# A DeltaNet layer's squares of q summed by column-group products, one head's transposes a unit later, and a selection matrix built earlier

## The chip, the cores and the metric

The kernel runs on one core of a Trainium2 chip. The time is the device time of one execution in microseconds (us), the median of several runs. The core's engines, as the profile names them: PE is TensorE (matmuls and transposes), PEld its weight loads, DVE is VectorE, ACT is ScalarE, POOL is GpSimd, SP is SyncE, which issues most of the DMAs.

## The reference

A decoder trunk of two layers over 512 positions of 1024 channels, float32. Layer 0 mixes tokens with a gated DeltaNet (8 heads of 128), layer 1 with a Conformer convolution. Each layer then attends to a fixed memory of 256 positions and applies a squared-ReLU MLP of width 4096. What the change touches, cut:

```python
def l2_normalize(x):
    return x * lax.rsqrt(jnp.sum(x * x, axis=-1, keepdims=True) + 1e-6)

# gated_deltanet
qkv = jax.nn.silu(causal_depthwise_conv(qkv, w_conv))
q = l2_normalize(q) * (DN_HEAD_DIM ** -0.5)
k = l2_normalize(k)
o = chunk_gated_delta_rule(q, k, v, g, beta)
o = o * lax.rsqrt(jnp.mean(o * o, axis=-1, keepdims=True) + RMS_EPS) * out_norm

# conformer_conv
u = h @ w_pw1 + b_pw1
u = u[..., :D_MODEL] * jax.nn.sigmoid(u[..., D_MODEL:])
c = causal_depthwise_conv(u, w_dw) + b_dw          # width 31
c = jax.nn.silu(layer_norm(c, ln_g, ln_b))
return c @ w_pw2 + b_pw2
# every sub-layer has rms_norm(h, g) before it
```

The division by q's length isn't applied to q. It goes into the RMS norm of o, as an addend: `o_norm` adds q's sum of squares (times a constant, in `ssq`) to the mean of o's squares before the root. So q's sums are needed only late.

## The kernel before, in words

Activations are kept transposed: a tile holds 128 channels (partitions) by 512 positions. Each weight half (128x1024) is loaded by SP, split into a high part `wh` by ACT (line 253) and a low part `wl` by DVE (or, for some, POOL) (line 73), and used in three matmuls (`mm3`, lines 300 to 302). Large activation tiles are split the same way (`xh`, `xl`). So TensorE waits whenever a split is late.

The order on each engine is written by a planner that takes the code's order as priority, and starts what is ready by its own model of times. Most tiles of 128x512 come from one pool of 69 slots (`slot`), the 8 PSUM banks from another (`psum`), and an instruction isn't ready before its slot is free. `keep_in_program_order` (also `pin`) ties an instruction behind all that was written before it for its engine; `issue_after` ties a block behind one instruction.

**DeltaNet.** `run(mains, sides)` issues a list of TensorE units (`mains`, half a projection tile each, some 2.7 to 3 us) and after each the small works planned for it (`sides`; `S.at(unit, rank, work)`). Units 4 to 33 are k, q, z and v of the first four heads (`gq` 0), 34 to 65 of the other four (`gq` 1), 66 to 73 the memory's keys (K's units), 74 to 81 its values (V's units), 82 to 89 half the output projection. The works that matter here:
- `q2` makes q times k of a head (units `Q2`) and keeps q as `self.QT[h]`, channels by positions.
- `q3` (units `Q3`) transposes q of a head in four matmuls into PSUM (`qt`), and ACT squares each of the four blocks with a running sum into a column of `ssq`, positions in the partitions. `norm_q` (units 33 and 62) adds an epsilon and scales.
- `fs_*` solve the triangular blocks on DVE; `mg_*` (units from 36 and from 68) merge them on TensorE.
- `tap_v`, `silu` make v of a head; `v2` transposes v (`vt`) and DVE scales it (`vb`). For `gq` 1 heads 4 to 6 go at unit 73, head 7 at unit 74. From unit 75 `rec` runs the recurrence, whose first matmul `vn` (unit 76) reads `vb`.
- `o_norm` (units 74 and 88) reads `ssq`.

The product `ab` at the start (line 1744) has four 32-column weights in TensorE's four column groups, each with a 128x512 tile.

**The first MLP's end and the conformer's start.** `mlp7(0)` forms its down projection in seven products per group of weights (`dn7`). Before the last group (`g == 3`) it calls `mid`, which splits the memory for layer 1 (`mem_gain`: `mh` by ACT, `ml` by DVE) and loads nine pieces of `taps`. `outs` then transposes the sums back (`hT`), adds the residual (`h`), splits it for the next norm (`parts`: `xh` by ACT, `xl` by DVE) and squares it (`Norm.square`), first for tiles 0 to 3 and, as `rest`, for 4 to 7, inside the conformer's first projection `pw_mm`. `norm.stat` multiplies the sum of squares by ones (`ssq`, line 442) at step `STAT` of the projection's eight, and ACT and DVE make `rb` from it, which `pw_ev` needs.

`sel`, made on DVE at the conformer's start from the identity, selects and sums rows in the layer norm after the convolution (`ln`).

Of the kernel before, what the change touches and what calls it, by code (L numbers as in the profile page):

```python
# [38 lines left out]
def tile_trunk(ctx, tc, xT, memT, x_d, mem_d, prm_d, adt_d, bdw_d, tap_d, fin_d, first_d, w_ab, w_kq, w_v, w_z, w_dno, w_pw1, w_pw2,  # L39
               w_q, w_k, w_vv, w_o, w_up, w_dn, yT):  # L40
    nc = tc.nc
    pe, act, dve, pool = nc.tensor, nc.scalar, nc.vector, nc.gpsimd
# [24 lines left out]
    def const(shape, s, dt=F32):  # L67
        return cp.tile(list(shape), dt, tag=s, name=s)
# [3 lines left out]
    def tt(e, o, a, b, op):  # L72
        r = e.tensor_tensor(out=o, in0=a, in1=b, op=op)  # L73
        if e is pool:
            last_pool[:] = [r]
        return r
# [4 lines left out]
    def ts(e, o, a, s1, op0, s2=None, op1=None):  # L81
        if op1 is None:
            return e.tensor_scalar(out=o, in0=a, scalar1=s1, scalar2=None, op0=op0)
        return e.tensor_scalar(out=o, in0=a, scalar1=s1, scalar2=s2, op0=op0, op1=op1)

    def c4(t):
        return t.rearrange("p (c i) -> p c i", c=4)
# [4 lines left out]
    def over_c(t, n=4):  # L92
        return t.unsqueeze(1).to_broadcast([P, n, t.shape[1]])
# [18 lines left out]
    def piece(e, i):  # L112
        e.dma_start(out=raw0[:, i * 256:(i + 1) * 256], in_=w_kq[0][:, i * 256:(i + 1) * 256])
# [11 lines left out]
    ident = const([P, P], "ident")  # L125
# [4 lines left out]
    for i in range(WARM):  # L130
# [5 lines left out]
    pool.affine_select(out=tri_gt, in_=ones, pattern=[[-1, P]], compare_op=ALU.is_gt, fill=0.0,  # L136
                       base=0, channel_multiplier=1)
    piece(act, 1)
    ones_r = const([P, P], "ones_r", F32R)
    pool.tensor_copy(ones_r, ones)  # L140
    tri_mid = const([P, P], "tri_mid")
# [58 lines left out]
    for kind, gq in DN_ORDER:  # L200
        for i in range(2):
            j = gq * 2 + i
# [202 lines left out]

    class Norm:
        def __init__(self, gname):
            self.g, self.acc, self.xs, self.n, self.side = gname, None, [], 0, None

        def add(self, t, h):  # L410
            self.parts(t, h)
# [6 lines left out]
            pin(stt(xl, h, pc(self.g, t), xh.bitcast(F32), ALU.mult, ALU.subtract))  # L418
            self.xs.append((xh, xl))

        def square(self, h, e=pool, side=False):
            sq = slot(s="sq")
            act.activation(sq, h, AF.Square)  # L423
            self.n += 1
            if side:
                if self.side:
                    tt(pool, self.side, self.side, sq, ALU.add)
                self.side = self.side or sq
                return
            if self.acc is None:  # L430
                self.acc = sq
            else:
                tt(dve if self.n == KT else e, self.acc, self.acc, sq, ALU.add)
            if self.n == KT:
                if self.side:
                    tt(dve, self.acc, self.acc, self.side, ALU.add)
                self.hl = split(self.acc, "sq")

        def stat(self):
# [28 lines left out]
    class DeltaNet:  # L468
# [196 lines left out]
            self.QT[h] = qT  # L665

        def q3(self, h):
            ps, sq = psum("qt"), slot(s="sqq")
            for c in range(4):
                cs = slice(c * P, (c + 1) * P)  # L670
                pe.transpose(ps[:, cs], self.QT[h][:, cs], ident)
            for c in range(4):
                cs = slice(c * P, (c + 1) * P)
                act.activation(sq[:, cs], ps[:, cs], AF.Square, accum_out=self.ssq[:, 4 * h + c:4 * h + c + 1])

        def norm_q(self, gq):
            v = self.ssq[:, 16 * gq:16 * gq + 16]
            ts(dve, v, v, EPS, ALU.add, EPS * P, ALU.mult)


        def fs_in(self, h):
# [291 lines left out]
    def mem_gain(layer, half):  # L973
        gn = f"xa_mem{layer}"
        if half == 0:
            mem["xs"] = []
        for j in (2 * half, 2 * half + 1):
            if layer == 1:
                m = mem["m"][j].rearrange("p (k t) -> p k t", k=2)
                tt(dve, m, m, over_c(mem["rs"][:, 0:256], 2), ALU.mult)  # L980
            mh = slot(F32R, "mh")
            ml = slot(F32R, "ml")
            for i in range(2):
                ks = slice(i * 256, (i + 1) * 256)
# [181 lines left out]
    def mlp7(layer, norm, hres, nxt=None, mid=None):  # L1166
# [123 lines left out]
        new = [None] * 8  # L1290

        def outs(tiles):
            todo = [(n, c, i) for n in range(2) for c in range(2) for i in tiles]
            pss = {i: psum("hT") for i in tiles}
            for n, c, i in todo:
                j = 2 * n + c
                pe.transpose(pss[i][:, j * P:(j + 1) * P], acc[n, 1 - i // 4, c][:, i % 4 * P:i % 4 * P + P], ident)
            for k, i in enumerate(tiles):
                hn = slot(s="h")
                tt(dve, hn, pss[i], hres[i], ALU.add)  # L1300
                new[i] = hn
                if k:
                    nxt.parts(i - 1, new[i - 1])
                if i > 5:
                    nxt.square(new[i - 2], side=True)
            nxt.parts(i, hn)
            for hn in new[0:4] if i == 3 else new[6:8]:
                nxt.square(hn, pool if i == 3 else dve)

        def final(n, m, c, held=None):  # L1310
            opens = n not in fin or fin[n][4][c] is None
# [92 lines left out]
    def taps(m, *pieces):  # L1404
        TAPS.setdefault(m, [])
        for i in pieces:
            t = slot(s="tap")
            nc.sync.dma_start(out=t, in_=tap_d[m - NTAP, i])
            TAPS[m].append(t)

    def conformer(norm, hres, nxt, rest):
        xs = norm.xs
        st, x16 = {}, {}
# [2 lines left out]
        Yp = [fsp.tile([P, 1024], F32, tag="fs", name=nm("cyp")) for _ in range(2)]  # L1416
        bias = slot(s="bdw")[:, 0:P]
        nc.sync.dma_start(out=bias, in_=bdw_d)
        sel = slot(s="sel")
        dve.tensor_reduce(out=sel[:, 128:160], in_=ident.rearrange("p (g t) -> p t g", g=4), op=ALU.add, axis=AX.X)  # L1420
        dve.tensor_reduce(out=sel[:, 160:164], in_=c4(ident), op=ALU.add, axis=AX.X)
        dve.tensor_copy(c4(sel[:, 0:128]), over_c(sel[:, 128:160]))
        own, same_t = over_c(sel[:, 160:164]), sel[:, 0:128]

        def pw_mm(i, hf):
# [242 lines left out]
        new = []  # L1668
# [21 lines left out]
    for i in range(4):  # L1690
        s = slice(i * 256, (i + 1) * 256)
# [30 lines left out]
    D = DeltaNet(n0)  # L1722
    D.decay_const(0)
    mains, S = [], Sides()
# [70 lines left out]
    for gq in range(2):  # L1795
        f0, nf = FS[gq]
        S.at(f0, 5, D.fs_begin, gq)
        for i in range(nf):
            S.at(f0 + i, 6, D.fs_steps, gq, i * 31 // nf, (i + 1) * 31 // nf)
        S.at(f0 + nf, 1, D.fs_end, gq)  # L1800
        for h in range(4 * gq, 4 * gq + 4):
            S.at(f0 + nf, 1, D.mg_a, h)
        S.at(f0 + 1, 7, D.norm_k, gq)
        S.at(f0 + nf + 2, 7, D.norm_q, gq)
        for i in range(4):
            h = 4 * gq + i
            S.at(f0 + nf - 4 + i, 5, D.mg_pre, h)
        a, b = (4 * gq, 4 * gq + 1), (4 * gq + 2, 4 * gq + 3)
        for j, (f, x, y) in enumerate(((D.mg_wy, a, ()), (D.mg_wy, b, a), (D.mg_te, a, ()), (D.mg_te, b, a), (D.mg_te, (), b))):
            S.at(MG[gq] + j, 1, f, x, y)  # L1810
        S.at(MG[gq] + 2, 1, D.mg_wy, (), b)
        for j, x in ((1, a), (2, b)):
            S.at(MG[gq] + j, 1.5, D.mg_u, x)
        for c in range(4):
            u = at["v", 4 * gq + 3] + V2[gq]
            if gq == 1:
                S.at(u, 3, D.v2, gq, c, (0, 1, 2))
                S.at(u + 1, 0, D.v2, gq, c, (3,))
        n = 0
        for c in range(4):  # L1820
            for step in range(3):
                S.at(REC[gq] + n, 0, D.rec, gq, c, step)
                n += 1
            S.at(REC[gq] + n + (c < 3 if gq == 1 else -(c == 1)), 5, D.o_gate, gq, c)
        S.at(ONORM[gq], 1, D.o_norm, gq)
    S.at(MSQ - 4, 7, mem_tok)
    for j in range(4):
        S.at(MSQ + j, 7, mem_square, j)
# [33 lines left out]
    h = []  # L1862
# [12 lines left out]
    n2 = Norm("mlp_norm0")  # L1875
    h = xattn(0, n1, h, n2)
    n3 = Norm("cv_norm")
    h, rest = mlp7(0, n2, h, n3, lambda: (mem_gain(1, 0), mem_gain(1, 1), taps(NTAP, *range(9))))
    n4 = Norm("xa_norm1")
    h = conformer(n3, h, n4, rest)  # L1880
    n5 = Norm("mlp_norm1")
# [3 lines left out]
    mlp7(1, n5, h)  # L1885


NSLOT = 69
NCV = 6
NRAW = 3  # L1890
RAWB = 6
# [21 lines left out]
ROOT_K = (32, 72)  # L1913
K2 = (15, 16, 18, 19, 45, 46, 49, 48)
Q2 = (18, 20, 22, 23, 48, 50, 50, 53)
Q3 = (24, 25, 27, 29, 55, 56, 57, 59)
FS = ((22, 9), (52, 8))
MG = (36, 68)
V2 = (10, 9)
# [6 lines left out]
TAPK = {0: 8, 1: 9, 2: 11, 3: 12}  # L1926
TAPQ = {0: 12, 4: 44}
TAPV = (37, 38, 39, 40, 69, 69, 70, 71)
STAT = 2
TAPS_U = (4,) * 7 + (6,) * 9 + (3,) * 8 + (0,) * 8  # L1930
TAPS_C = {4: 0, 5: 0, 6: 0, 7: 0}
SHARE = 5
# [113 lines left out]
```

## Time and profile before

| | us |
|---|---|
| median of 3 runs (1444.9 to 1445.53) | 1445.21 |
| the profiled execution | 1444.54 |
| its span, first to last instruction | 1442.8 |
| PE busy | 1432.4 |
| DVE busy | 1053.5 |
| ACT busy | 763.6 |
| POOL busy | 249.2 |

Lines of the profile give a start in us from the span's start, a duration in us, the engine, the source line (a helper such as line 73 or 79 stands for many callers), the operation, and out<-in by tile names. In brackets stands how long the engine was idle before and what released it. The duration of a matmul is longer than the step from one to the next, because they are pipelined.

### The profile page before, as it was taken

To read this page: it belongs to the slowest core of one execution; us is meant where nothing else is said; L and a number is where in the kernel's file an instruction comes from. 1 tells how busy PE (TensorE), PEld (TensorE's weight loads), DVE (VectorE), ACT (ScalarE), POOL (GpSimd) and SP (SyncE) were. 2 spreads that over 40 slices of the span, in tenths; PEclk is the share of its full clock that TensorE was granted. 3 is DMA by queue.
4 is the path that set the end of the run, shared out by engine and by line. 5 is a ranking of instruction groups with operands and counts; after the bars stand their busy time and mean duration, and the time that the engine had idled before them with its cause. 6 is when DMAs were issued, how large, how long until landed. Compare 5 with 4: busy or idle time off the path is not lost.

```text
span 1442.8 us, 20243 instructions
## 1 busy us (share of the span) xinstructions
PE 1432.4 (99%) x7670; PEld 1199.2 (83%) x7670; DVE 1053.5 (73%) x1600; ACT 763.6 (53%) x1322; POOL 249.2 (17%) x250
## 2 busy tenths in 40 slices
PE   9999999999999999999999999999999999999998
PEld 7888889888888888888888778888888888888886
DVE  6989888867555765767679899975555766767677
ACT  6767856655444454434355655564444544444354
POOL 1301200102113010010100478111112010010101
PEclk9999999999999999999999999999999999999999
DMA  8232225522214576575766448743215476675853
GB/s 300 73 117 75 70 92 162 195 84 88 74 40 127 153 177 175 141 206 131 198 165 217 141 147 244 252 139 99 73 49 141 117 182 169 149 206 135 222 150 88
DMA packets 71857, 207.80 MB, mean 144 GB/s; under 512 B 15440, under 2 KB 16592, under 8 KB 71760
## 3 DMA queue, kind: packets, MB, share of 16 engines
q1 hardware_dynamic: 60960, 169.22, 35.9%
q0 software_dynamic: 9792, 35.66, 14.5%
q10 hardware_dynamic: 1008, 1.64, 0.3%
q8 instruction: 60, 0.98, 0.3%
q14 instruction: 37, 0.30, 0.1%
HBM read 203.28 MB, written 3.21 MB: 143 GB/s over the span
## 4 chain that ended last, share of the span: by engine, by line
PE 91%; DVE 5%; ACT 2%; issue 1%; DMA 0%; POOL 0%; SPq 0%; DVEq 0%; ACTq 0%; POOLq 0%
PE up L302 8%; PE up L301 8%; PE up L300 8%; PE dn L1218 7%; PE dn L1217 7%; PE dn L1216 7%; PE h L300 3%; PE h L302 3%; PE h L301 3%; PE xo L301 2%; PE q L301 2%; PE xo L300 2%; PE q L300 2%; PE q L302 2%; PE xo L302 2%; PE pw L302 2%
## 5 line engine op out<-in xcount | busy, mean ns | idle before, releaser
L253 ACT CAST wh<-raw 128x1024 fp32r<-128x1024 f32 x259 | 271.6, 1051 | 345.0 <-issue 89.1
L73 DVE TENSOR_TENSOR wl<-raw,wh 128x1024 fp32r<-128x1024 f32 (+1 forms) x250 | 306.0, 1225 | 97.1 <-ACT wh L253 94.8
L300 PE MATMUL up<-xh,wh 128*128 128x512 f32 x512 | 199.7, 390 | 0.0
L302 PE MATMUL up<-xh,wl 128*128 128x512 f32 x512 | 199.3, 389 | 0.0
L301 PE MATMUL up<-xl,wh 128*128 128x512 f32 x512 | 199.2, 389 | 0.0
L302 PEld LDWEIGHTS up<-xh,wl 128*128 128x128 f32 x512 | 96.1, 188 | 19.9
L300 PEld LDWEIGHTS up<-xh,wh 128*128 128x128 f32 x512 | 96.1, 188 | 19.9
L301 PEld LDWEIGHTS up<-xl,wh 128*128 128x128 f32 x512 | 96.1, 188 | 19.9
L241 POOL DMA_DIRECT2D t<-w_dn x48 | 42.1, 914 | 367.5 <-DVE wl L73 269.6
L1216 PE MATMUL dn<-wh,ah 128*128 128x512 f32 (+1 forms) x260 | 100.5, 387 | 0.0
L1218 PE MATMUL dn<-wl,ah 128*128 128x512 f32 (+1 forms) x260 | 100.4, 386 | 0.0
L1217 PE MATMUL dn<-wh,al 128*128 128x512 f32 (+1 forms) x260 | 100.4, 386 | 0.0
L79 DVE SCALAR_TENSOR_TENSOR rl<-up,rb 128x512 f32<-128x512 f32 x64 | 44.1, 689 | 58.4 <-PE up L302 58.4
L253 ACT CAST wh<-t 128x1024 fp32r<-128x1024 f32 x44 | 46.4, 1054 | 55.0 <-PE dn L1217 43.7
L73 DVE TENSOR_TENSOR wl<-t,wh 128x1024 fp32r<-128x1024 f32 x44 | 53.6, 1223 | 28.7 <-ACT wh L253 28.6
L73 POOL TENSOR_TENSOR sq<-sq,sq 128x512 f32<-128x512 f32 x28 | 46.0, 1643 | 154.2 <-ACT sq L423 143.6
L1495 DVE SCALAR_TENSOR_TENSOR ca<-xn,prm,ca 128x512 f32<-128x512 f32 x85 | 64.1, 754 | 5.7 <-ACT ca L1492 3.4
L73 DVE TENSOR_TENSOR acc<-acc,dn 128x512 f32<-128x512 f32 x99 | 66.6, 682 | 1.0
L300 PE MATMUL h<-xh,wh 128*128 128x512 f32 x160 | 64.2, 401 | 0.0
L302 PE MATMUL h<-xh,wl 128*128 128x512 f32 x160 | 62.5, 390 | 0.0
L301 PE MATMUL h<-xl,wh 128*128 128x512 f32 x160 | 62.4, 390 | 0.0
L73 DVE TENSOR_TENSOR al<-u,ah 128x512 fp32r<-128x512 f32 x64 | 44.1, 688 | 21.4 <-ACT ah L359 21.4
(421 smaller groups left out, 3520.2 us busy)
## 6 DMA issues: line engine op xcount, KB each, us to landing
raw<-w_dn SPq DMA_DIRECT2D x68, 512.0 KB, 4.5
raw<-w_up SPq DMA_DIRECT2D x64, 512.0 KB, 4.8
t<-w_dn POOLq DMA_DIRECT2D x48, 512.0 KB, 6.4
tap<-tap SPq DMA_DIRECT2D x48, 256.0 KB, 6.2
raw<-w_pw SPq DMA_DIRECT2D x24, 512.0 KB, 4.6
raw<-w_dn POOLq DMA_DIRECT2D x20, 512.0 KB, 6.6
raw<-w_k SPq DMA_DIRECT2D x16, 512.0 KB, 4.1
raw<-w_vv SPq DMA_DIRECT2D x16, 512.0 KB, 6.1
```

The lines of the kernel that those rows point to most:

```text
L73: r = e.tensor_tensor(out=o, in0=a, in1=b, op=op)
L79: return dve.scalar_tensor_tensor(out=o, in0=a, scalar=s, in1=b, op0=op0, op1=op1)
L241: nc.gpsimd.dma_start(out=t, in_=a, accum_op=ALU.add)
L253: ins = [act.copy(h, raw)]
L300: pe.matmul(ps, wh, xh, start=first, stop=False)
L301: pe.matmul(ps, wh, xl, start=False, stop=False)
L302: pe.matmul(ps, wl, xh, start=False, stop=last)
L1216: pe.matmul(ps, xh, w[0][:, s], start=opens and k == 0, stop=False, skip_group_check=True)
L1217: pe.matmul(ps, xl, w[0][:, s], start=False, stop=False, skip_group_check=True)
L1218: pe.matmul(ps, xh, w[1][:, s], start=False, stop=k == 3, skip_group_check=True)
L1495: first["tap"] = dve.scalar_tensor_tensor(out=a, in0=src, scalar=w, in1=a, op0=ALU.mult, op1=ALU.add)
```

## The change

The squares of q are taken by ACT from the channel-by-position tile, without transposing it. Two rounds of four products (`q_sums`, at units `QS` = 32 and 66) sum them over the channels: the weight `selq` has 16 columns of ones and 16 of zeros, and head j of the four goes to column group j, so that a round fills rows of one 128x512 bank. The first matmul of a round is pinned behind all that TensorE was given before, the others follow it in order. The second round lands in other rows and is added by DVE. At unit 71 `q_turn` transposes the sum (four matmuls), and two DVE operations write `ssq`. `norm_q` goes. Head 7 in `v2` moves from unit 74 to 75. The side sum on POOL in `Norm.square` goes: of the conformer's eight squares POOL adds numbers 0 to 2 and DVE 3 to 7. `norm.stat` there moves one step later. `sel` is made in `mid`. The pool has 70 slots.

```diff
+    selq = const([P, 48], "selq")
+    pool.memset(selq, 1.0)
+    pool.memset(selq[:, 16:32], 0.0)
...
-        def square(self, h, e=pool, side=False):
+        def square(self, h, e=pool):
             sq = slot(s="sq")
             act.activation(sq, h, AF.Square)
             self.n += 1
-            if side:
-                if self.side:
-                    tt(pool, self.side, self.side, sq, ALU.add)
-                self.side = self.side or sq
-                return
             if self.acc is None:
                 self.acc = sq
             else:
                 tt(dve if self.n == KT else e, self.acc, self.acc, sq, ALU.add)
             if self.n == KT:
-                if self.side:
-                    tt(dve, self.acc, self.acc, self.side, ALU.add)
                 self.hl = split(self.acc, "sq")
...
         def q3(self, h):
-            ps, sq = psum("qt"), slot(s="sqq")
+            sq = self.M["sq", h] = slot(s="sqq")
+            act.activation(sq, self.QT[h], AF.Square)
+
+        def q_sums(self, gq):
+            ps = psum("qq")
+            for j in (3, 2, 1, 0):
+                with nullcontext() if j == 3 else tc.issue_after(ins.ins):
+                    ins = pe.matmul(ps[32 * j:32 * j + 32, :], selq[:, 16 * gq:16 * gq + 32], self.M.pop(("sq", 4 * gq + j)),
+                                    start=True, stop=True)
+                if j == 3:
+                    tc.keep_in_program_order(ins)
+            if gq == 0:
+                self.qq = slot(s="qq")
+                act.copy(self.qq, ps)
+            else:
+                tt(dve, self.qq, self.qq, ps, ALU.add)
+
+        def q_turn(self):
+            ps = psum("qt")
             for c in range(4):
                 cs = slice(c * P, (c + 1) * P)
-                pe.transpose(ps[:, cs], self.QT[h][:, cs], ident)
-            for c in range(4):
-                cs = slice(c * P, (c + 1) * P)
-                act.activation(sq[:, cs], ps[:, cs], AF.Square, accum_out=self.ssq[:, 4 * h + c:4 * h + c + 1])
-
-        def norm_q(self, gq):
-            v = self.ssq[:, 16 * gq:16 * gq + 16]
-            ts(dve, v, v, EPS, ALU.add, EPS * P, ALU.mult)
+                pe.transpose(ps[:, cs], self.qq[:, cs], ident)
+            v = self.ssq.rearrange("p (g j c) -> p g j c", g=2, j=4)
+            for gq in range(2):
+                ts(dve, v[:, gq], ps.rearrange("p (c j g x) -> p g j c x", c=4, j=4, g=2)[:, gq, :, :, 0],
+                   EPS, ALU.add, EPS * P, ALU.mult)
...
-                if i > 5:
-                    nxt.square(new[i - 2], side=True)
             nxt.parts(i, hn)
-            for hn in new[0:4] if i == 3 else new[6:8]:
-                nxt.square(hn, pool if i == 3 else dve)
+            for k in range(3) if i == 3 else range(3, 8):
+                nxt.square(new[k], pool if i == 3 else dve)
...
+    def selections():          # the three lines that stood in conformer(), called at the end of mid
...
-        S.at(f0 + nf + 2, 7, D.norm_q, gq)
+        S.at(QS[gq], 3, D.q_sums, gq)
...
-                S.at(u + 1, 0, D.v2, gq, c, (3,))
+                S.at(u + 2, 0, D.v2, gq, c, (3,))
...
+    S.at(QS[1] + 5, 3, D.q_turn)
...
-NSLOT = 69
+NSLOT = 70
-Q3 = (24, 25, 27, 29, 55, 56, 57, 59)
+Q3 = (27, 28, 28, 29, 56, 57, 58, 59)
+QS = (32, 66)
-STAT = 2
+STAT = 3
```

More of the change, by code (lines that the diff above doesn't have):

```diff
@@ L407, in __init__ @@
         def __init__(self, gname):
-            self.g, self.acc, self.xs, self.n, self.side = gname, None, [], 0, None
+            self.g, self.acc, self.xs, self.n = gname, None, [], 0
         def add(self, t, h):
@@ L1409, in taps @@
             TAPS[m].append(t)
+    SEL = []
+    def selections():
+        sel = slot(s="sel")
+        dve.tensor_reduce(out=sel[:, 128:160], in_=ident.rearrange("p (g t) -> p t g", g=4), op=ALU.add, axis=AX.X)
+        dve.tensor_reduce(out=sel[:, 160:164], in_=c4(ident), op=ALU.add, axis=AX.X)
+        dve.tensor_copy(c4(sel[:, 0:128]), over_c(sel[:, 128:160]))
+        SEL.append(sel)
     def conformer(norm, hres, nxt, rest):
@@ L1418, in conformer @@
         nc.sync.dma_start(out=bias, in_=bdw_d)
[L1419 to L1422, printed above, removed]
+        sel = SEL[0]
         own, same_t = over_c(sel[:, 160:164]), sel[:, 0:128]
@@ L1877, in tile_trunk @@
     n3 = Norm("cv_norm")
-    h, rest = mlp7(0, n2, h, n3, lambda: (mem_gain(1, 0), mem_gain(1, 1), taps(NTAP, *range(9))))
+    h, rest = mlp7(0, n2, h, n3, lambda: (mem_gain(1, 0), mem_gain(1, 1), taps(NTAP, *range(9)), selections()))
     n4 = Norm("xa_norm1")
```

## The prediction, made before the changed kernel was run

> **What bounds the kernel now.** I read first the page's head, the busy table and the chain that ended last. Columns of the table: busy time, share of the span, instructions.
>
> ```profile
> span 1442.8 us, 20243 instructions
> PE 1432.4 (99%) x7670; PEld 1199.2 (83%) x7670; DVE 1053.5 (73%) x1600; ACT 763.6 (53%) x1322; POOL 249.2 (17%) x250
> PE 91%; DVE 5%; ACT 2%; issue 1%; DMA 0%; POOL 0%; SPq 0%; DVEq 0%; ACTq 0%; POOLq 0%
> ```
>
> TensorE is the bound: 91% of the chain. So an edit is worth what it takes from TensorE's queue, or a wait of TensorE that it takes away; work of the other engines counts only where TensorE waits for it. Next I read the weight loader's waits in the stretch from 750 to 850 us: they name where DVE or POOL is late, in total, times and longest.
>
> ```profile
> PEld pw L301 <- DVE xl L79: 2.6, 4, 1.1
> PEld pw L302 <- POOL xn L1445: 0.9, 1, 0.9
> PEld dn L1218 <- DVE wl L73: 0.6, 1, 0.6
> ```
>
> The change touches the first (the conformer's opening) and the third (the MLP's last group). Then I read timelines: start, duration, engine, line, tiles. A matmul's duration overlaps the next one, so costs are differences of starts.
>
> **1. Squares of q on TensorE.** The parts that go: 8 times four transposes of `qt`. One set, on PE:
>
> ```profile
> 84.01 0.40 PE L354 MATMUL z<-wh,xl 128*128 128x512 f32 x1
> 84.25 0.60 PE L671 MATMUL qt<-ident,cva 128*128 128x128 f32 x4
> ...
> 84.92 0.40 PE L353 MATMUL z<-wl,xh 128*128 128x512 f32 x1
> ...
> 12.86 0.51 PE L1740 MATMUL h<-xl,wh 128*128 128x512 f32 x1
> 13.30 1.06 PE L1744 MATMUL ab<-x,abp 128*32 128x512 f32 x8
> 14.30 0.50 PE L1738 MATMUL h<-xh,wh 128*128 128x512 f32 x1
> 14.64 0.40 PE L1739 MATMUL h<-xh,wl 128*128 128x512 f32 x1
> ```
>
> From 84.01 to 84.92 are 0.91 us; the two 512-column matmuls alone would need two pitches of 0.23 (84.01 to 84.25 is one). So a set costs 0.45, and eight cost 3.6. The parts that come: two rounds of `q_sums`, each four products of a 128x32 weight with a 128x512 float32 tile into the four column groups. The trace has that very form in `ab` (second part of the fence): 12.86 to 14.64 are 1.78, less two pitches 1.32. Two rounds cost 2.64. `q_turn` adds one set of four transposes, 0.45. Net -3.6 + 2.64 + 0.45 = -0.5 us.
>
> A float32 product is two instructions, so a round is eight; they are through in 1.00 (13.30 to 14.30), which I read as two passes of 0.5 with the four groups side by side, and the other 0.32 as entry and exit. The Trainium skill, TensorEngine Tiling (Array Packing), Key Properties, says that a change of the tiling mode drains TensorE, which speaks against a small grouped round between full-width matmuls. The trace agrees by that 0.32 of 1.32. By the same page's Theoretical Speedup alone (four column tiles in the time of one) a round would be an estimated 1.0, its two passes, and the net -1.1; the `ab` row decides.
>
> **2. Squares of q elsewhere.** ACT did four reads with sums per head out of PSUM; now it does one 128x512 square from SBUF per head, like `sq` of the opening (0.62, part 4). ACT is not late there, so this is worth 0; if ACT became late, the silus of q and k would be the next late work, and this edit only frees it. The first round's copy (ACT, by the same row some 0.6) lies in v's units, where TensorE doesn't wait for it. In K's units DVE gets one add of 128x512 with an input in PSUM (0.69, as `vb` in part 3) and two small `ts` for the two that go. DVE is late there, as the next part shows, and `mg` is next in its queue:
>
> ```profile
> 239.43 0.69 DVE L726 STREAM_TRANSPOSE x<-u 128x512 f32<-128x512 f32 x1
> ...
> 240.88 0.69 PE L748 MATMUL mg<-x,bt 32*32 32x32 f32 x32
> ```
>
> `mg` needs that transpose, done at 240.12: 0.76 to spare. The first round and four sets less put TensorE 0.5 earlier against DVE, and the add, should it stand ahead, takes 0.69: a wait of 0.4 at worst, 0 at best. I take 0.1. The four squares and the sum `qq` hold slots longer (`qq` from unit 32 to 71, with one slot more in all); nothing in the trace prices that, the bounds are 0 and one evicted tile's wait as in part 3 (0.76). I take 0, because the squares go when their round has run.
>
> **3. `vt`'s last head one unit later.** PE and the releaser:
>
> ```profile
> 263.86 0.39 PE L354 MATMUL V<-wh,ml 128*128 128x512 f32 x1
> ...
> 264.80 0.66 PE L818 MATMUL vt<-ident,cva 128*128 128x128 f32 x4 [0.55 <-ACT cva L613]
> 265.21 0.47 PE L352 MATMUL V<-wh,mh 128*128 128x512 f32 x1
> 265.53 0.39 PE L353 MATMUL V<-wl,mh 128*128 128x512 f32 x1
> 266.31 0.69 DVE L73 TENSOR_TENSOR vb<-vt,nk 128x512 f32<-128x512 f32 x1 [0.49 <-ACT nk L809]
> ```
>
> 263.86 to 265.53 are 1.67; a set of transposes without a wait is 0.91: TensorE loses 0.76 here to the silu of v's last head. One V unit is 12 matmuls, 2.7 us, so at unit 75 the silu is long done: -0.76. What is late next: `vb` (four times 0.6), now some 2.7 us later, and its reader `vn` at the end of unit 76. The first `vb` needs 0.69 of the 2.7 us between; `vn` doesn't wait unless DVE has two weight splits ahead of it. 0.
>
> **4. The conformer's opening.** The squares of tiles 0 to 7 used two sums (POOL's side sum for 4 and 5); now POOL adds 0 to 2 and DVE adds 3 to 7. `sel`'s three operations leave DVE here. TensorE, then DVE and POOL:
>
> ```profile
> 793.60 1.36 PE L1297 MATMUL hT<-ident,acc 128*128 128x128 f32 x11
> 797.35 0.39 PE L302 MATMUL pw<-xh,wl 128*128 128x512 f32 x1
> 797.58 0.39 PE L300 MATMUL pw<-xh,wh 128*128 128x512 f32 x1
> 798.62 0.50 PE L301 MATMUL pw<-xl,wh 128*128 128x512 f32 x1 [0.66 <-DVE xl L79]
> ...
> 803.66 0.39 PE L300 MATMUL pw<-xh,wh 128*128 128x512 f32 x1
> ...
> 794.03 0.38 DVE L1420 TENSOR_REDUCE sel<-ident 128x32 f32<-128x128 f32 x1
> 795.26 1.28 DVE L73 TENSOR_TENSOR h<-hT,h 128x512 f32<-128x512 f32 x2
> 795.34 2.68 POOL L73 TENSOR_TENSOR sq<-sq,sq 128x512 f32<-128x512 f32 x2
> 796.74 1.83 DVE L79 SCALAR_TENSOR_TENSOR xl<-h,prm,xh 128x512 fp32r<-128x512 f32 x1 [0.19 <-ACT xh L416]
> 797.22 0.62 ACT L423 ACTIVATE sq<-h 128x512 f32<-128x512 f32 x1
> 799.09 0.73 DVE L79 SCALAR_TENSOR_TENSOR xl<-h,prm,xh 128x512 fp32r<-128x512 f32 x1
> 800.35 2.44 DVE L79 SCALAR_TENSOR_TENSOR xl<-h,prm,xh 128x512 fp32r<-128x512 f32 x2
> 800.52 1.73 POOL L73 TENSOR_TENSOR sq<-sq,sq 128x512 f32<-128x512 f32 x1 [2.50 <-ACT sq L423]
> 802.72 2.27 DVE L73 TENSOR_TENSOR sq<-sq,sq 128x512 f32<-128x512 f32 x3
> ```
>
> From 797.58 to 803.66 TensorE starts 18 matmuls; at 0.227 they need 4.09, so 6.08 - 4.09 = 2.0 us are waits for `xl`. Three things make `xl` late. `sel` holds DVE from 794.03 to 795.26, while the first tile's transposes are done about 794.6 (the eleven end at 794.96, the last of tile 4 is three earlier): 0.6. The first `xl` takes 1.83 instead of 0.73 and ends (798.57) 0.55 after POOL's third add (795.34 + 2.68 = 798.02). The last `xl` is slow again beside POOL's side add at 800.52 (the two take 2.44, not 1.4). So DVE's `xl` stands still while POOL reads SBUF. The Trainium skill, SBUF — State Buffer, Who interferes with whom, states it: "A DVE instruction with two SBUF inputs contends with a GpSimd instruction that reads SBUF", and the later one blocks; the trace agrees with 1.83 against 0.73.
>
> With the change: the adds of `h` start at 794.65, the first `xl` at 796.13 (1.48 later, as before); POOL's second and now last add ends at 795.34 + 1.34 = 796.68, and 0.55 after that `xl` is done: 797.2 instead of 798.57. The next two follow at the old steps (1.25, 1.3), 798.45 and 799.75, the last in 0.73: 800.55 instead of 802.8. TensorE, not waiting, wants them with the matmul 1, 4, 9 and 15 pitches of 0.227 after 797.58 (from the third on it takes two tiles in turn): 797.8, 798.5, 799.6 and 801.0. The third is 0.15 late, and a restart costs 0.1: some 0.3 of waits is left and 1.7 go. Bounds: 2.0, and 1.0 if one of the five new DVE adds (0.7) is put between the `xl` and costs a restart. I take 1.7.
>
> The sum of squares: DVE's adds go from three (2.27) to five, 5 x 0.79 = 3.95 from 800.55, done at 804.5 against 804.99 before. Half a microsecond earlier, and its matmul, one `k` later (`STAT` 3, +0.68) but 1.7 earlier with TensorE, wants it 1.0 earlier:
>
> ```profile
> 806.04 0.68 DVE L73 TENSOR_TENSOR sql<-sq,sqh 128x512 fp32r<-128x512 f32 x1
> 807.07 0.40 PE L442 MATMUL ssq<-sqh,ones_r 128*128 128x512 f32 x1
> ...
> 816.60 0.69 DVE L73 TENSOR_TENSOR sg<-pw,rb 128x512 f32<-128x512 f32 x1 [1.68 <-PE pw L302]
> ```
>
> The second `ssq` matmul (0.23 after the first) had 807.30 - 806.72 = 0.58 to spare; 0.1 is left. 0, at worst 0.5. The gain holds after that: at 816.60 DVE's next tile waits 1.68 for TensorE, not for `rb`, so the 0.68 of `STAT` is absorbed, and the wait for POOL's `xn` stays what it was.
>
> **5. `sel` in the MLP's last group.** Its three operations now come after `mem_gain` and the taps in the order in which the planner takes ready work, and before the splits of the group's later weights. There DVE is full:
>
> ```profile
> 757.93 2.88 DVE L79 SCALAR_TENSOR_TENSOR ml<-mem,prm,mh 128x256 fp32r<-128x256 f32 x7
> 760.73 1.22 DVE L73 TENSOR_TENSOR wl<-raw,wh 128x1024 fp32r<-128x1024 f32 x1
> ...
> 762.00 0.50 PE L1218 MATMUL dn<-wl,sh 128*128 128x512 f32 x1 [0.15 <-DVE wl L73]
> ```
>
> TensorE already waits for this `wl`. If `sel` (795.26 - 794.03 = 1.23) goes ahead of it, that wait grows by 1.23; if it finds its slot only after the split, or a gap of DVE, it costs 0. Both are possible, the last tap (and with it the slot behind it) comes at about the time of that split; I take half, +0.6.
>
> The two fills of `selq` on POOL at the start are behind nothing that is awaited: 0.
>
> **Sum.** -0.5 (q) + 0.1 (`mg`) - 0.76 (`vt`) - 1.7 (opening) + 0.6 (`sel`) = -2.3 us. The profiled execution took 1444.54 around its span of 1442.8, 0.67 under the median 1445.21 of the runs. Against the median: 1442.9.
>
> **The rivals.** *`sel` is the new wait.* It stands ahead of the split and costs its whole 1.23 (perhaps with the leftover `ml` behind it), and a DVE add is put between the `xl`: -0.5 - 0.76 - 1.0 + 1.23 + 0.1 = -0.9: 1444.3. For it: DVE has no idle time from 757.93 on. Against: the planner could place it earlier, slots allowing. *All of it lands.* `sel` in a gap, 2.0 at the opening: -0.5 - 0.76 - 2.0 = -3.3: 1441.9. Against: the third `xl` still comes late by the steps above. *A round is not one of column groups at once.* If the pinned order makes the eight passes of a round follow one another, a round costs 8 x 0.5 + 0.32 = 4.3 instead of 1.32, and two add 6.0: 1448.9, slower. For it: every product is two passes, and the pin fixes the order in which they are queued. Against: `ab`'s eight run in 1.06. It decides from a round of 2.5 on, where the whole gain is gone. In this case the change doesn't do what it says, make q's sums cheaper.
>
> **How the numbers follow.** My forecast (1441.9 to 1444.0 by its own terms) 0.5; `sel` as a wait 0.2; all of it 0.2; serial rounds 0.05; orders elsewhere that shift with the slots, either way, 0.05. 0.2% is 2.9 us, about what a measurement of this kernel can tell from no change; faster than that is 1442.3 or less: most of "all of it" and a fifth of the forecast, 0.3. Slower than 1448.1 needs serial rounds or worse: 0.06. The range leaves out serial rounds and takes in all else: 1441.0 to 1445.8.
>
> **What would show it.** `qt` x4 instead of x32 and two groups of eight 128*32 matmuls of about 1.06; no wait before `vt`; `xl` at about 0.73 each with no POOL add beside the later ones, and waits of `pw` for `xl` under 0.5; `sel` near 760, and whether `dn L1218` waits longer than 0.6 there. I'd be wrong if `ssq`, `mg` or `vn` show a wait of a microsecond, or if a round takes over 2 us.

## The result, and the profile after

| | before | after |
|---|---|---|
| median of 20 runs each, us | 1444.99 (1444.52 to 1446.13) | 1442.78 (1442.18 to 1444.49) |
| ratio | | 0.9985, 95% interval 0.9978 to 0.9992 |
| span of the profiled execution | 1442.8 | 1442.0; a second profile of the same kernel 1440.2 |

The change is worth 2.2 us (1.2 to 3.2 by the interval); the forecast was 2.3, to 1442.9. The page's head and the busy table of the changed kernel:

```profile
span 1442.0 us, 20172 instructions
PE 1431.3 (99%) x7658; PEld 1196.4 (83%) x7658; DVE 1052.0 (73%) x1603; ACT 760.7 (53%) x1267; POOL 245.9 (17%) x250
```

TensorE is the bound as before. The first profile is 1.8 longer than the second (`after_again` below), nearly all of it from the start: near 24.7 TensorE waited for `rstd` of the first norm, for which ACT, just before, had waited as long for a DMA of `x`.

```profile
PE rb L403 <- DVE rstd L448: 1.0, 1, 1.0
```

Whether this late start has to do with the edit stays open. Of the nine profiles here of the changed kernel and its variants it shows in five (TensorE waits 0.4 to 1.0 for `rstd`), and in none of the five others, among them the kernel with q's part alone, which has the same two fills of `selq` at the start.

Sums are made against the second profile, which doesn't have it, and the method is this: the start of one and the same matmul in two profiles, subtracted. Where that difference steps, an edit has gained or lost. All terms, in us:

| step | forecast | second profile of after against before |
|---|---|---|
| eight sets of `qt` go | -3.6 | -3.85 (-1.91, -1.94) |
| two rounds | +2.64 | +2.40 (1.22, 1.18) |
| `q_turn` | +0.45 | +0.40 |
| waits of `mg` | +0.1 | +0.50 |
| wait for a weight split in K's units | 0 | +0.40 |
| `vt` | -0.76 | -0.78 |
| opening of the conformer | -1.7 | -1.70 |
| `sel` in the MLP's last group | +0.6 | 0 |
| sum | -2.3 | -2.63 |

The span fell by 2.6 (1442.8 to 1440.2); small steps elsewhere, -0.15 before 70 us and +0.15 in all later, cancel. The median of the runs fell by 2.2; the two agree within the interval. From 70 us on, behind its late start, the first profile gains 2.3 against the kernel before; it waits 0.3 longer at `mg`.

**The rounds.** Operations on the tiles `qq` (count, shortest, median and longest ns, first and last start), then TensorE's timeline round the first round:

```profile
L671 PE MATMUL qq<-sqq,selq x16: 592/605/617, 107.6 to 235.3; 128*32 128x512 f32 x16
L685 PE MATMUL qt<-ident,qq x4: 272/273/331, 254.7 to 255.1; 128*128 128x128 f32 x4
```

```profile
107.23 0.39 PE L305 MATMUL h<-xh,wl 128*128 128x512 f32 x1
107.55 1.06 PE L671 MATMUL qq<-sqq,selq 128*32 128x512 f32 x8
108.55 0.50 PE L303 MATMUL h<-xh,wh 128*128 128x512 f32 x1
108.88 0.39 PE L304 MATMUL h<-xl,wh 128*128 128x512 f32 x1
```

`qt` is four instructions instead of 32, and a round is one group of eight that runs in 1.06. From 107.23 to 108.88 are 1.65; less two pitches of 0.23 a round costs 1.19, of which 1.00 (107.55 to 108.55) is its two passes. So entry and exit are 0.19, where `ab` at the start had 0.32. The Trainium skill, TensorEngine Tiling (Array Packing), Key Properties, says that a change of the tiling mode drains TensorE; the 0.19 a round agrees with that.

**The waits behind the rounds.** PE and its weight loader between 100 and 280 us, first profile, then ACT's timeline at the first `mg`, one row of the kernel before and two of the second profile:

```profile
PE mg L759 <- ACT w L769: 0.5, 1, 0.5
PEld K L305 <- DVE wl L73: 0.3, 1, 0.3
```

```profile
121.45 0.78 ACT L758 ACTIVATE w<-mg 32x256 f32<-32x256 f32 x2
...
120.56 0.73 ACT L597 ACTIVATE cva<-cv,prm 128x512 f32<-128x512 f32 x1 [2.74 <-DVE cv L73]
121.31 0.78 ACT L769 ACTIVATE w<-mg 32x256 f32<-32x256 f32 x2
```

ACT's `w`, which `mg` needs, is queued behind a `cva`, and that waited 2.74 for DVE's `cv`. In the kernel before, `w` was done at 122.23 and `mg` read it at 122.45: 0.2 to spare. With the change `w` is done at 122.09, hardly earlier, while TensorE is 0.7 earlier (-1.91 and +1.22), so it waits 0.5. So it is DVE that is late, as the prediction had it, but TensorE waits 0.5 and not 0.1, and a second place is late that the prediction did not have: a split `wl` of K's weights. DVE there, one row of the kernel before, then the first profile of the change:

```profile
236.28 1.18 DVE L73 TENSOR_TENSOR wl<-raw,wh 128x1024 fp32r<-128x1024 f32 x1
...
236.85 0.65 DVE L73 TENSOR_TENSOR qq<-qq,qq 128x512 f32<-128x512 f32 x1
...
241.75 1.23 DVE L73 TENSOR_TENSOR wl<-raw,wh 128x1024 fp32r<-128x1024 f32 x1
```

The add didn't just push the split back by its 0.65. In the kernel before, the split stood at this place, 4.4 before TensorE read it (at 241.85); with the add there, the planner put the split behind the copies and transposes for `mg`, in a stretch (227 to 244) in which DVE has no pause.

**`vt`.** The set of head 7 has no wait any more: 268.28 to 269.19 are the 0.91 that the prediction named.

```profile
268.28 0.40 PE L357 MATMUL V<-wh,ml 128*128 128x512 f32 x1
268.51 0.60 PE L829 MATMUL vt<-ident,cva 128*128 128x128 f32 x4
...
269.19 0.39 PE L356 MATMUL V<-wl,mh 128*128 128x512 f32 x1
```

**The opening.** The same two matmuls that stood at 797.58 and 803.66, then DVE and POOL:

```profile
798.36 0.39 PE L303 MATMUL pw<-xh,wh 128*128 128x512 f32 x1
...
802.75 0.39 PE L303 MATMUL pw<-xh,wh 128*128 128x512 f32 x1
...
794.08 3.36 POOL L73 TENSOR_TENSOR sq<-sq,sq 128x512 f32<-128x512 f32 x2
...
796.98 1.01 DVE L79 SCALAR_TENSOR_TENSOR xl<-h,prm,xh 128x512 fp32r<-128x512 f32 x1 [0.20 <-ACT xh L419]
798.52 0.74 DVE L79 SCALAR_TENSOR_TENSOR xl<-h,prm,xh 128x512 fp32r<-128x512 f32 x1
799.78 1.62 DVE L79 SCALAR_TENSOR_TENSOR xl<-h,prm,xh 128x512 fp32r<-128x512 f32 x2
```

The 18 matmuls take 4.39 instead of 6.08; at 0.227 they need 4.09, so 0.30 of waits is left, and 1.7 went. The first `xl` ends (797.99) 0.55 after POOL's last add (794.08 + 3.36 = 797.44), the distance that the trace of before had. The weight loader's waits from 750 to 850:

```profile
PEld dn L1229 <- DVE wl L73: 0.6, 1, 0.6
PEld pw L304 <- DVE xl L79: 0.6, 2, 0.3
PEld ssq L438 <- DVE sql L73: 0.2, 1, 0.2
```

**`sel`** (operations on the tile): not near 760, but behind the split that the prediction feared for, and the wait of `dn` is the same 0.6.

```profile
L1424 DVE TENSOR_REDUCE sel<-ident x1: 397/397/397, 767.7 to 767.7; 128x32 f32<-128x128 f32 x1
...
L1426 DVE COPY sel<-sel x1: 225/225/225, 768.2 to 768.2; 128x128 f32<-128x128 f32 x1
```

### The profile page after: what moved, and what is told of

The parts are those of the page before. It is cut to its first block, busy times and chain, and to the rows that moved or that the text cites. A ratio compares the mean times of both kernels' runs of the same rounds, so it can differ in the third digit from the quotient of the medians.

```text
span 1442.0 us, 20172 instructions
## 1 busy us (share of the span) xinstructions
PE 1431.3 (99%) x7658; PEld 1196.4 (83%) x7658; DVE 1052.0 (73%) x1603; ACT 760.7 (53%) x1267; POOL 245.9 (17%) x250
## 3 DMA queue, kind: packets, MB, share of 16 engines
q10 hardware_dynamic: 1008, 1.64, 0.3%
## 4 chain that ended last, share of the span: by engine, by line
PE 85%; DVE 9%; ACT 2%; DMA 1%; issue 1%; POOL 1%; SPq 0%; ACTq 0%; DVEq 0%; POOLq 0%
PE up L303 8%; PE up L304 8%; PE up L305 8%; PE dn L1229 7%; PE dn L1228 7%; PE dn L1227 7%; PE pw L304 2%; PE pw L303 2%; PE pw L305 2%; DVE wl L73 2%; PE xo L304 2%; PE q L303 2%; PE xo L303 2%; PE q L304 2%; PE q L305 2%; PE xo L305 2%
## 5 line engine op out<-in xcount | busy, mean ns | idle before, releaser
L73 POOL TENSOR_TENSOR sq<-sq,sq 128x512 f32<-128x512 f32 x26 | 42.8, 1646 | 151.6 <-ACT sq L426 137.4
```

## The experiments

Each kernel was timed beside the kernel before on the same chip; us are medians, and the interval of a ratio is about ±1.3 us. Where less is at issue the profile's starts decide, and the text says so.

### One part of the change at a time

**q alone** (kernel before with `selq`, the new `q3`, `q_sums`, `q_turn`, `Q3`, `QS` and 70 slots):

```diff
-        S.at(f0 + nf + 2, 7, D.norm_q, gq)
+        S.at(QS[gq], 3, D.q_sums, gq)
...
+    S.at(QS[1] + 5, 3, D.q_turn)
...
-NSLOT = 69
+NSLOT = 70
```

> The kernel before with the squares of q alone changed (q3, q_sums, q_turn, 70 slots). Theory: TensorE's own work falls by 0.5 us as costed, but the merges now wait because DVE's solve keeps its time while TensorE arrives earlier: about 0.8 at the first merge and 0.4 in K's units, as in the profile of the changed kernel. Net +0.7 us, 1445.7; the wait stands before an mg matmul near 123. Rival: that wait is an accident of the one profiled execution, as its late start is; then -0.5 us, 1444.5, and no wait at mg.

Measured: 1444.38 against 1444.90, ratio 0.9996 [0.9987, 1.0005]. The median is the rival's -0.5, the profile's sum the theory's +0.7: sets -3.85, rounds +2.38, `q_turn` +0.39, the wait in K's units +0.4, and two waits of `mg` that cost 1.7 together (the rows below), of which `vt`, now later, gives 0.34 back. The first wait (0.8 in all) and that in K's units are the theory's. The second (0.9) is not, and the profile names nothing that ended it ("issue"), so the sum came out at +0.7 partly by luck. That execution was 0.5 over its own median. So the first wait and K's are real, but their size changes from one execution to the next by more than the part is worth; whether q alone gains or loses half a microsecond stays open.

```profile
PE mg L766 <- issue: 0.7, 1, 0.7
PE mg L766 <- ACT w L776: 0.5, 1, 0.5
```

**Head 7 of v alone:**

```diff
-                S.at(u + 1, 0, D.v2, gq, c, (3,))
+                S.at(u + 2, 0, D.v2, gq, c, (3,))
```

> The kernel before with head 7 of vt one unit later and nothing else. Theory: the wait of 0.76 before vt goes and nothing takes its place: -0.76 us. Rival: the wait of vt only moves on, to vb and vn, or DVE's next split is late instead: 0.

Measured: 1444.37 against 1444.90, 0.9995 [0.9987, 1.0004]. In the profile the wait for `vt` is gone (-0.78 there), and 0.16 of it comes back at `vn`, whose weight loader waits 0.3 for `vb`. So its cover is thin, and what the prediction called 0 is nearly spent.

```profile
PEld vn L868 <- DVE vb L73: 0.3, 1, 0.3
```

**The opening's squares alone** (without `sel`):

```diff
-            for hn in new[0:4] if i == 3 else new[6:8]:
-                nxt.square(hn, pool if i == 3 else dve)
+            for k in range(3) if i == 3 else range(3, 8):
+                nxt.square(new[k], pool if i == 3 else dve)
...
-STAT = 2
+STAT = 3
```

> The kernel before with the sums of squares at the conformer's opening alone changed (no side sum on POOL, three squares on POOL, five on DVE, STAT 3); sel stays at the opening. Theory: POOL's third and side adds stood in the way of xl; without them the last xl is done near 800.8 instead of 802.8, and about 0.5 of the 2.0 us of waits is left: -1.5 us. Rival: sel's 1.2 us of DVE at that place was the larger part; then it still holds the first xl, and the gain is half, -0.8 or less.

Measured: 1443.97 against 1444.90, 0.9993 [0.9984, 1.0002]; in the profile -1.45 at the opening, the theory's size, while the medians (-0.9) can't tell it from the rival's. The weight loader's waits for `xl` fall from 2.6 to 0.8.

**`sel` alone** (with 70 slots):

```diff
-    h, rest = mlp7(0, n2, h, n3, lambda: (mem_gain(1, 0), mem_gain(1, 1), taps(NTAP, *range(9))))
+    h, rest = mlp7(0, n2, h, n3, lambda: (mem_gain(1, 0), mem_gain(1, 1), taps(NTAP, *range(9)), selections()))
```

> The kernel before with sel made in the MLP's last group (and 70 slots for it), nothing else. Theory: DVE begins the opening's h 0.6 earlier, but the first xl then waits for POOL's third add as before, so TensorE gains nothing there, and sel costs nothing where it now stands: 0, within 0.2. Rival: sel at the opening was worth its 0.6 on the path: -0.6. Second rival, the one of the prediction: it stands ahead of a weight split in the last group: +0.6 to +1.2, with the wait of dn for wl longer than 0.6.

Measured: 1444.34 against 1444.90, 0.9996 [0.9987, 1.0005]. In the profile -0.44 at the opening, and `dn` waits as long as before, so the first rival is nearer. Weight loader, 750 to 850:

```profile
PEld pw L301 <- DVE xl L79: 1.8, 2, 1.1
...
PEld dn L1218 <- DVE wl L73: 0.6, 1, 0.6
```

By the profiles the opening is -1.45 without `sel`'s move, -0.44 with it alone, and -1.70 with both: the two shorten partly the same wait.

### What the rounds cover

**The change again:** no edit. Its second profile is the one in the table.

> The changed kernel as it is, for a second profile beside this call's kernels. Theory: its late start (TensorE waiting 1.0 for rstd near 25 us, behind a late load of x) is an accident of that one execution and is not there, while the waits before mg at 123 (0.8) and for wl in K's units (0.3 to 0.4) are its plan's and stand again. 1442.8. Rival: the late start belongs to the change (two more fills on POOL at the start), and stands again.

Measured: 1442.67 against 1444.83, 0.9986 [0.9977, 0.9994]. The late start is gone, and the wait of `mg` is smaller than in the first profile:

```profile
PE mg L759 <- ACT w L769: 0.2, 1, 0.2
```

**The first round eight units later**, behind the first `mg`:

```diff
-QS = (32, 66)
+QS = (40, 66)
```

> The changed kernel with its first round at unit 40, behind the merges, instead of 32, before them. Theory: before the merges TensorE has lost 1.9 us of transposes while DVE's solve keeps its time, and the round's 1.2 covers most of that; behind the merges it covers nothing, so the wait at mg grows from 0.8 to about 2.0 and the kernel loses about 1.0: 1443.8. Rival: the wait at mg comes from ACT's copy of the round's sum, which stands before the merges' copies; then the wait goes, and the time falls by 0.8: 1442.0.

Measured: 1443.69 against 1444.83, 0.9994 [0.9985, 1.0003], by the medians 1.0 slower than the change measured beside it, which is within the intervals; its span is 1.4 longer than that of the change's second profile, 0.5 of it from the start. TensorE comes to `mg` a round earlier and waits for it:

```profile
PE mg L759 <- ACT w L769: 1.3, 1, 1.3
```

From the last matmul before this `mg` to the first behind it TensorE loses 1.64 against the kernel before, and 0.49 in the second profile of the change: the 1.2 of the round is nearly all cover there. This is the theory's wait, and the rival's ACT copy did not matter. So the first round costs little where it stands, because TensorE without it would wait for DVE, and this is also why the transposes that went brought less than their price.

**`mg` one unit later:**

```diff
-MG = (36, 68)
+MG = (37, 69)
```

> The changed kernel with both merges one unit later (37 and 69 instead of 36 and 68). Theory: a unit is 2.7 us, more than DVE is late, so the waits before mg go: 0.8 at 123, perhaps the 0.3 in K's units, and nothing behind them waits for the merged blocks before unit 45: -0.8 us, 1442.0. Rival: the recurrence and the splits of K's units are next in DVE's and ACT's queues and wait instead: 0 or slower.

Measured: 1446.97 against 1444.83, 1.0016 [1.0007, 1.0025]: 4.3 slower than the change. My theory, that a unit more removes the waits, fell. The waits grow:

```profile
PE mg L759 <- ACT w L769: 2.0, 1, 2.0
PE mg L792 <- ACT w L801: 1.0, 2, 0.6
PE K L305 <- DVE wl L73: 0.9, 1, 0.9
```

In the change `w` follows the first `cva` on ACT at once (120.56 and 121.31 above). Here one more `cva` (at 125.27, after 2.65 of waiting for DVE's `cva`) and a weight's `wh` (at 125.81) stand in front of `w` (126.86): moved by a unit, it comes behind more of the other works.

**Without the pin** (`q_sums` with neither `keep_in_program_order` nor `issue_after`):

```diff
-                with nullcontext() if j == 3 else tc.issue_after(ins.ins):
-                    ins = pe.matmul(ps[32 * j:32 * j + 32, :], selq[:, 16 * gq:16 * gq + 32], self.M.pop(("sq", 4 * gq + j)),
-                                    start=True, stop=True)
-                if j == 3:
-                    tc.keep_in_program_order(ins)
+                pe.matmul(ps[32 * j:32 * j + 32, :], selq[:, 16 * gq:16 * gq + 32], self.M.pop(("sq", 4 * gq + j)),
+                          start=True, stop=True)
```

> The changed kernel with the four products of a round neither pinned nor tied to each other. Theory: the planner starts each as soon as its square is there, between wide matmuls, so they no longer run side by side: one product alone is two passes, about 1.0, plus 0.3 for entry and exit, so up to 4 x 1.3 = 5.2 a round instead of 1.3, and the kernel is slower by up to 8 us (1450), by 3 if only one of four leaves its round. Rival: the planner keeps the four together by itself: 0.

Measured: 1443.13 against 1444.83, 0.9987 [0.9978, 0.9996], no difference from the change that could be told. The theory fell and the rival was right: the planner keeps the eight together by itself:

```profile
106.02 1.06 PE L670 MATMUL qq<-sqq,selq 128*32 128x512 f32 x8
```

**The second round's add on POOL instead of DVE:**

```diff
-                tt(dve, self.qq, self.qq, ps, ALU.add)
+                q2 = slot(s="qq")
+                act.copy(q2, ps)
+                tt(pool, self.qq, self.qq, q2, ALU.add)
```

> The change, but the second round of q's sums is copied out of PSUM by ACT and added to the first by POOL, instead of the add on DVE (0.65 at 236.85). Theory: DVE has no idle time from 227 to 246 in the changed kernel, so what it is given there comes straight back as TensorE's wait for `wl` of K (0.4 at 242); without the add the wait goes, and the kernel is 0.4 faster than the change (2.6 faster than before). POOL has no instruction between 236 and 250 and ACT is idle 1.15 before 237.02. Rival: ACT's copy (0.6) stands ahead of its copies of `UB`, from which DVE makes the tiles of `mg`, and POOL's add, which reads two tiles of SBUF, slows DVE; then the wait moves to `mg` (0.3 to 0.6 at 244) and nothing is gained.

Measured: 1442.82 against 1444.93, 0.9987 [0.9978, 0.9996], as the change. The theory was right in its place: the planner puts a split where the add stood (234.92), no wait for `wl` of K is left, and TensorE is 0.42 earlier from 242 on. But 0.3 of it comes back at 269, where the first matmul of the recurrence waits for `vb`. DVE and POOL of this kernel, and the weight loader's wait:

```profile
234.92 1.18 DVE L73 TENSOR_TENSOR wl<-raw,wh 128x1024 fp32r<-128x1024 f32 x1
...
240.24 1.28 POOL L73 TENSOR_TENSOR qq<-qq,qq 128x512 f32<-128x512 f32 x1 [14.31 <-ACT qq L680]
240.33 2.27 DVE L73 TENSOR_TENSOR wl<-raw,wh 128x1024 fp32r<-128x1024 f32 x1
...
248.58 4.07 DVE L79 SCALAR_TENSOR_TENSOR cva<-cv,prm,cva 128x512 f32<-128x512 f32 x6 [1.92 <-ACT cva L597]
...
268.78 2.47 DVE L73 TENSOR_TENSOR vb<-vt,nk 128x512 f32<-128x512 f32 x4
```

```profile
PEld vn L881 <- DVE vb L73: 0.4, 1, 0.4
```

DVE has a pause at 248, for ACT's `cva`; in the change's second profile it ends at 248.48, 0.1 sooner. From there to `vb` (268.67 in the change) DVE is idle only 0.65 here, and it is no earlier for the add that went, while TensorE is 0.36 earlier. So what TensorE gains at 242 it mostly gives back at `vn`. The rival was right that POOL's add slows DVE (the split at 240.33 takes 2.27 instead of 1.2), but that held up nothing, and not `mg`.

### The opening, one step back at a time

**A third add given to POOL:**

```diff
-            for k in range(3) if i == 3 else range(3, 8):
+            for k in range(4) if i == 3 else range(4, 8):
```

> The change, with one add of the conformer's squares given back to POOL: POOL adds 0 to 3 (three adds), DVE 4 to 7. Theory: `xl` stands still while POOL reads SBUF. In the changed kernel POOL's two adds end at 797.44 and the first `xl` at 797.99, 0.55 behind. A third add of about 1.34 ends at 798.8, so the first `xl` (0.73 on its own) is done about 799.3, with some 2 us instead of 1.01; TensorE waits about 1.3 more for `xl` in all, and the kernel is about 1.2 slower than the change: 2.2 faster than before becomes 1.0 faster. Rival: what made `xl` late in the kernel before was `sel` in front of it and the side sum at the end, not the third add; then the first `xl` stays near 1.0, the waits near 0.6 in total, and the kernel is as fast as the change, or 0.1 faster by DVE's add that goes.

Measured: 1443.10 against 1444.93, 0.9988 [0.9979, 0.9996]: 0.4 less gain than the change had, within the interval, and in the profile 0.45 lost at the opening and 0.3 more at `ssq`. The direction is the theory's, the size some two thirds by the profile.

```profile
793.33 5.07 POOL L73 TENSOR_TENSOR sq<-sq,sq 128x512 f32<-128x512 f32 x3
...
796.23 1.02 DVE L79 SCALAR_TENSOR_TENSOR xl<-h,prm,xh 128x512 fp32r<-128x512 f32 x1 [0.20 <-ACT xh L419]
797.17 0.68 DVE L73 TENSOR_TENSOR h<-hT,h 128x512 f32<-128x512 f32 x1
797.77 1.18 DVE L79 SCALAR_TENSOR_TENSOR xl<-h,prm,xh 128x512 fp32r<-128x512 f32 x1
```

POOL's adds end at 793.33 + 5.07 = 798.40, and the second `xl` ends (798.95) 0.55 behind that. The first one still ends at 797.25: it did not wait for the third add but got in between, 0.55 after the end of the second (796.70). `xl` waits for the add that is running, not for all that POOL has queued. The add of `h` from PSUM keeps its 0.68 beside POOL. The Trainium skill, SBUF — State Buffer, Who interferes with whom, says that the order of issue decides who blocks; this trace agrees.

**`sel` back at the conformer's start:**

```diff
+        selections()
         sel = SEL[0]
...
-taps(NTAP, *range(9)), selections()))
+taps(NTAP, *range(9))))
```

> The change, but `sel` is made at the conformer's start, as before. Theory: `sel`'s three operations (1.23 in the kernel before) stand in front of the first add of `h` on DVE and make the first `xl` some 0.5 later; the wait for `wl` of `dn` in the MLP's last group stays at 0.6, as it does with `sel` there. So 0.45 slower than the change (what moving `sel` alone gave at the opening): 1.75 faster than before. Rival, the prediction's step: `sel` costs the MLP 0.6 by making `wl` of `dn` wait, and the wait falls here to 0; then the kernel is 0.1 to 0.2 faster than the change.

Measured: 1443.32 against 1444.93, 0.9988 [0.9979, 0.9997]: 0.6 less gain than the change had, within the interval; 0.31 in the profile, all of it at the opening, and the wait of `dn` is again 0.6. So the theory, with two thirds of its size.

```profile
793.62 3.37 POOL L73 TENSOR_TENSOR sq<-sq,sq 128x512 f32<-128x512 f32 x2
...
794.38 0.38 DVE L1424 TENSOR_REDUCE sel<-ident 128x32 f32<-128x128 f32 x1
794.68 0.28 DVE L1425 TENSOR_REDUCE sel<-ident 128x4 f32<-128x128 f32 x1
794.88 0.82 DVE L1426 COPY sel<-sel 128x128 f32<-128x128 f32 x1
...
797.09 0.75 DVE L79 SCALAR_TENSOR_TENSOR xl<-h,prm,xh 128x512 fp32r<-128x512 f32 x1 [0.19 <-ACT xh L419]
```

It is less than `sel`'s length because the first `xl`, now later, falls behind POOL's adds and takes its own 0.75.

**`STAT` 2:**

```diff
-STAT = 3
+STAT = 2
```

> The change with `STAT` 2 as before: the product that sums the squares over the channels stands one step (0.68) earlier in TensorE's queue. Theory (the prediction had 0.1 to spare with 3; the profile of the change has a wait of 0.2 there): the wait of `ssq` for DVE's split `sql` grows from 0.2 to 0.9, and the kernel is 0.7 slower than the change, 1.5 faster than before. Rival: DVE's adds are placed earlier when the sum is wanted earlier, and the wait stays under 0.4; then no difference.

Measured: 1443.23 against 1444.93, 0.9986 [0.9977, 0.9995]: 0.5 less gain than the change had by the medians, within the interval, and 0.43 in the profile. The theory in direction, with some two thirds of its size.

```profile
PEld ssq L438 <- DVE sql L73: 0.6, 1, 0.6
```

No version here beats the change. The change with 69 slots was not tried, so what the slot is worth stays open.

## Why the prediction came out, point by point

The total was right, and that is partly luck: four terms were off by 0.4 to 0.6 each, two in either direction, and their errors nearly cancel.

- **q's rounds and sets.** Forecast -0.5 net, measured -1.05 (-3.85 + 2.40 + 0.40). A set costs 0.48 instead of 0.45 and a round 1.19 to 1.22 instead of 1.32; `ab`, the nearest row, has dearer entry and exit than a round has here. The serial rounds did not come, with or without the pin.
- **`mg`, +0.1.** This step was mis-sized. The prediction counted the 0.5 by which TensorE comes earlier net, and put it against 0.76 to spare at the second `mg`. But the four sets of `qt` go before each round, 1.9, and the first `mg`, for which it had looked up no margin, has only 0.2: TensorE, 0.7 earlier there, loses 0.5 (0.8 in the first profile). Moving the first round away showed the mechanism: TensorE's waits grow by what it comes earlier, since DVE delivers at its own pace there.
- **K's units, 0.** This step failed in what it looked at. The add was set against `mg` alone; but it took the place of a weight split, which the planner then put behind the work for `mg`, and TensorE waits for that split, +0.4. With the add on POOL the split went back to its place and this wait went, and 0.3 came back at `vn`.
- **`vt`, -0.76, next wait 0.** -0.78. The cover of `vb` held in the change with about nothing to spare: `vn` waits 0.3 as soon as TensorE is 0.4 earlier.
- **The opening, -1.7 with 0.3 left.** Measured -1.70 with 0.30 left. The reason given, that `xl` stands still while POOL reads SBUF, holds by the third add given back to POOL. The five adds on DVE did not get between the `xl`; `ssq` has a wait of 0.2 where 0.1 was to be spare, and `STAT` 2 would have cost 0.43 more.
- **`sel`, +0.6.** This step failed: it was the mean of two cases, and the one in which it costs nothing came. The planner put it at 767.7, behind the split of 760.7. Its gain at the opening was counted, rightly, in the term above.

The rivals "all of it" (-3.3) and "`sel` is the new wait" (-0.9) are not what came: the opening gave 1.7, not 2.0, and `dn`'s wait did not move.

## What to carry to other kernels

When an edit takes work from the engine that is the bound, look up the margin of every place behind it where another engine delivers just in time, the first one too, and count the earliness at that place rather than the net of the whole edit: what is over the margin comes back as a wait, and if that wait is removed it may come back at the next such place. An added instruction is to be set against all that stands behind it in its queue up to the next pause, not against the next reader alone, and a planner may answer it by another order, so that what stood at its place comes much later. Parts of half a microsecond are not told apart by medians with an interval of ±1.3; the starts of the same instruction in two profiles tell them apart, and a second profile tells which differences belong to the execution.

## What the runs showed of the hardware

- A copy of 128x128 from SBUF to SBUF on DVE takes 0.225 with none of POOL's adds running (768.2 in the change) and 0.82 beside them (794.88 with `sel` back at the start), while the two reductions ahead of it take 0.28 to 0.40 in both places. The Trainium skill, SBUF — State Buffer, Who interferes with whom, states both: copies can contend with GpSimd, `tensor_reduce` on trn2 never does. The rows agree.
- The blocking goes both ways. In the kernel before and in the change POOL's first add starts while DVE splits a weight, an operation with two inputs in SBUF, and takes 1.99 instead of the 1.30 of the second. In the kernel before, the split ended at 794.11 and this add, the row below, at 795.26; in the change the two ended at 794.93 and 796.07. So the add ended 1.14 to 1.15 after the split.
- DVE's `xl` ended 0.54 to 0.55 after the end of the add that it had waited for, in all eight such rows of four traces (the kernel before, `sel` alone, the change and the third add given to POOL), less than the 0.73 it takes on its own; the blocked copy above ended 0.08 after the add. So the part that doesn't need POOL's reading to end, 0.1 to 0.2, seems to be done by then. That is a reading of rows, not an experiment.

```profile
793.27 1.99 POOL L73 TENSOR_TENSOR sq<-sq,sq 128x512 f32<-128x512 f32 x1
```
